# Attention weights, keys and queries turned by VectorE through DRAM, with all transfers of turned tiles issued by GpSimd

## The chip, the cores and the metric

The kernel runs on one core of one Trainium2 chip. The metric is the device time of one execution in microseconds (us). The engines of the core work beside each other, each in the order of its own instructions: TensorE (PE) multiplies matrices into PSUM banks, VectorE (DVE) and ScalarE (ACT) do the elementwise work, GpSimd (POOL) does small things, and SyncE (SP) issues loads. ACT, SP and now POOL also issue transfers (DMAs), which run on 16 DMA engines.

## What is computed

A backbone of two layers over 256 latent rows (4 grid rows of 64) and 256 context rows, with 2048 channels, in float32. The first layer has 16 attention heads beside 32 heads of a state-space scan (SSD), the second a short gated convolution. What the change touches is the attention of the first layer:

```python
def rms_norm(x, g):
    xf = x.astype(jnp.float32)
    y = xf * lax.rsqrt(jnp.mean(xf * xf, axis=-1, keepdims=True) + EPS)
    return (y * g.astype(jnp.float32)).astype(x.dtype)
...
    q = rms_norm(heads(cols(p, COL_Q, NA_WIDTH, 0), NA_HEADS, NA_HEAD_DIM), q_norm_g)
    k = rms_norm(heads(cols(p, COL_K, NA_WIDTH, 0), NA_HEADS, NA_HEAD_DIM), k_norm_g)
...
        s_lat = jnp.einsum('bqhd,bkhd->bhqk', qr, kb).astype(jnp.float32) * scale + bias.astype(jnp.float32)
        s_lat = jnp.where(mask, s_lat, -jnp.inf)
        s_ctx = jnp.einsum('bqhd,bkhd->bhqk', qr, k_ctx).astype(jnp.float32) * scale
        pr = jax.nn.softmax(jnp.concatenate([s_lat, s_ctx], axis=-1), axis=-1).astype(v.dtype)
...
    ya = neighbourhood_attention(q, k, v, k_ctx, v_ctx, rpb).reshape(b, seq, NA_WIDTH)
    ya = ya * jax.nn.silu(cols(p, COL_GATE_A, NA_WIDTH, 0))
```

Each head has 256 queries, 512 keys and a width of 128. Its 256 x 512 weights are taken times the values, the result times a SiLU gate.

## The kernel before

Every weight of the model is read once, in tiles of 128x1024 floats that SP loads into one of the `raw` buffers. ACT rounds a tile to `wH` (L423), DVE takes the rest as `wL` (L430), and PE multiplies three times, high by high, high by low and low by high (L198, the helper `mm`). Three pairs of `wH` and `wL` exist, so a pair can only be made over when PE is done with an older one. The input projection of the first layer runs through its columns in four stretches, each with four heads and two groups of the scan, then come the output projection, the second layer's input projection and its output projection.

Beside this stream stand generators: one for the keys or queries of four heads (`kq_gen`), one per head (`head_gen`), some per SSD group (`make_x`, `group_gen`), and one for the modulation's matrix-vector product (`gemv_gen`, on DVE, L820, from loads named `in_ada_w`). A planner, the class `Plan`, keeps a clock for each engine from a table of costs. While the stream of matmuls is written out, `pump` lets a generator go on as soon as its next instruction's inputs are ready by these clocks; so the table sets the order in which the work of the generators stands between that of the stream. What is written is a fixed order for each engine; nothing is reordered on the chip, and an engine whose next instruction waits does nothing behind it.

PE needs operands with the summed index on the 128 partitions. So K, Q and the attention weights have to be turned. Before, PE does it in steps of 128x128 (`turn`, L202, a multiplication with the identity that lands in a PSUM bank):

- `kq_gen` norms four tiles of 128x512 of K (two of Q) with DVE (L962), has each turned by four of PE's instructions, and copies the bank to `KT` with ACT (L979) or times the norms' gains to `QT` with DVE (L981).
- `head_gen` splits K and Q of the head in high and low parts, has the scores of 128 queries at a time multiplied (`kH,qH` and so on), adds the bias and takes the maximum on DVE (L1036), the exponential on ACT (L1041), divides on DVE (L1046), has 4 turns on PE, then splits the turned bank into `PH` (ACT, L1082) and `PL` (DVE, L1084). With `PH`, `PL` and the values PE makes the weighted sum.
- At the end of `group_gen` two 128x128 matmuls of a matrix of ones and a diagonal spread 256 norm factors `r` over the partitions; the factors come from a power on POOL (L1437).

The second layer already turns in another way: a row tile is written to DRAM (`trd`) by ACT's queue, fetched back in four transfers that place blocks of 32 on their partitions (`fetch`, L212), and DVE turns inside each 32x32 block (L217, STREAM_TRANSPOSE).

The results of heads and groups go to DRAM (`mixd`), and `mix_gen` reads them back for the output projection.

## Time and profile before

| | us |
|---|---|
| median of 3 runs | 1801.51 (1799.98 to 1804.06) |
| profiled execution | 1802.22 |
| its span, first to last instruction | 1800.3 |
| TensorE matmuls busy | 1760.2 |
| VectorE busy | 1283.5 |
| ScalarE busy | 785.7 |
| GpSimd busy | 31.1 |
| mean granted TensorE clock | 0.998 of full |

The span is shown in 40 slices of 45 us, each digit the busy share in tenths:

```profile
PE   6999999999999999999999999999999999999998
DVE  5566777878686867685875787787657777767555
DMA  9987654576656556655574566768757888878774
```

PE is busy in nearly every slice. The first two slices wait for the first loads, the last one holds the end of the output. DMA is the share in which the 16 DMA engines were busy: it is full at the start and between 0.5 and 0.7 during the attention (about 200 to 1150 us), and near 0.8 in the second layer (about 1370 us on).

### The profile page before, as it was taken

The page shows a single profiled execution, that of the slowest core. Times are in us where ns is not written, and L with a number is a line of the kernel's source. Part 1 is how long each engine was busy: PE and PEld are TensorE (multiplying, and loading weights), DVE is VectorE, ACT ScalarE, POOL GpSimd, SP SyncE. Part 2 cuts the span into 40 slices and gives each one's busy share as a digit, 9 for nine tenths or more (in the row PEclk, how much of TensorE's full clock was granted, in tenths as well). Part 3 has the DMA queues.
Part 4 walks back from the last instruction along what each step waited for, and adds up shares of the span by engine and source line. Part 5 has one row for each costly group of instructions (what it writes and reads, how often), then busy time and mean ns, then how long its engine had stood idle before and what let it go on. Part 6 is the DMA issues. An engine that isn't in the chain of part 4 may idle for free.

```text
span 1800.3 us, 25545 instructions
## 1 busy us (share of the span) xinstructions
PE 1760.2 (98%) x9545; PEld 1469.2 (82%) x9545; DVE 1283.5 (71%) x2049; ACT 785.7 (44%) x1354; POOL 31.1 (2%) x28
## 2 busy tenths in 40 slices
PE   6999999999999999999999999999999999999998
PEld 4677888889888879888878898788877888878887
DVE  5566777878686867685875787787657777767555
ACT  5323544436252455242454343554445444434442
POOL 0000100001000000000001000000000000000000
PEclk9999999999999999999999999999999999999999
DMA  9987654576656556655574566768757888878774
GB/s 347 340 291 254 194 168 126 156 206 194 211 161 190 162 174 204 191 158 167 172 219 120 163 188 194 232 209 295 273 184 232 260 278 268 270 237 265 220 220 167
DMA packets 260220, 385.23 MB, mean 214 GB/s; under 512 B 33424, under 2 KB 113008, under 8 KB 260096
## 3 DMA queue, kind: packets, MB, share of 16 engines
q1 hardware_dynamic: 239792, 366.64, 64.8%
q10 hardware_dynamic: 20304, 16.96, 3.1%
q8 instruction: 75, 1.23, 0.3%
q14 instruction: 49, 0.40, 0.1%
HBM read 372.89 MB, written 11.96 MB: 214 GB/s over the span
## 4 chain that ended last, share of the span: by engine, by line
PE 89%; DMA 4%; DVE 4%; issue 1%; ACT 1%; SPq 0%; POOL 0%; ACTq 0%; POOLq 0%; DVEq 0%
PE bank L198 86%; PE bank L202 3%; DMA raw<-in_ada_w 2%; DVE wL L430 2%; DMA tmp<-dram_csr 1%; DVE acc L820 0%; DMA raw<-in_w_in 0%; DMA Dg<-dram_trd 0%; ACT wH L423 0%; DMA tmp<-in_x 0%; DMA xs<-in_x 0%; DVE hL L769 0%; DVE tmp L1398 0%; DVE tmp L1217 0%; DMA Du<-dram_trd 0%
## 5 line engine op out<-in xcount | busy, mean ns | idle before, releaser
L423 ACT CAST wH<-raw 128x1024 fp32r<-128x1024 f32 (+1 forms) x440 | 459.5, 1045 | 707.4 <-PE bank L198 606.5
L430 DVE TENSOR_TENSOR wL<-raw,wH 128x1024 fp32r<-128x1024 f32 (+1 forms) x440 | 530.5, 1212 | 225.9 <-ACT wH L423 224.1
L198 PE MATMUL bank<-hH,wH 128*128 128x256 f32 (+1 forms) x1040 | 342.7, 330 | 0.9 <-ACT wH L423 0.9
L198 PE MATMUL bank<-hL,wH 128*128 128x256 f32 (+1 forms) x1040 | 336.8, 324 | 0.0
L198 PE MATMUL bank<-hH,wL 128*128 128x256 f32 (+1 forms) x1024 | 331.3, 324 | 1.5 <-DVE wL L430 1.5
L198 PE MATMUL bank<-wH,h 128*128 128x512 f32 x1024 | 318.7, 392 | 2.1 <-DVE h L1662 1.7
L198 PE MATMUL bank<-wH,hH 128*128 128x512 f32 x640 | 257.2, 402 | 4.8 <-ACT hH L763 2.6
L820 DVE SCALAR_TENSOR_TENSOR acc<-raw,csil,acc 128x512 f32<-128x512 f32 x256 | 191.7, 749 | 91.0 <-DMA raw<-in_ada_w 74.0
L198 PE MATMUL bank<-wL,hH 128*128 128x512 f32 x640 | 249.8, 391 | 0.3 <-DVE wL L430 0.3
L198 PE MATMUL bank<-wH,hL 128*128 128x512 f32 x640 | 249.5, 390 | 0.1
L198 PEld LDWEIGHTS bank<-wH,h 128*128 128x128 f32 x1024 | 193.0, 189 | 44.3 <-DVE h L1662 3.0
L198 PEld LDWEIGHTS bank<-hH,wH 128*128 128x128 f32 x1040 | 197.6, 190 | 18.7 <-issue 2.0
L198 PEld LDWEIGHTS bank<-hL,wH 128*128 128x128 f32 x1040 | 197.7, 190 | 15.6
L198 PEld LDWEIGHTS bank<-hH,wL 128*128 128x128 f32 x1024 | 194.5, 190 | 17.8 <-DVE wL L430 2.5
L198 PE MATMUL bank<-wL,h 128*128 128x512 f32 x512 | 200.7, 392 | 5.4 <-DVE wL L430 5.4
L198 PE MATMUL bank<-wH,mix 128*128 128x512 f32 x512 | 162.7, 393 | 0.0
L198 PEld LDWEIGHTS bank<-wH,hH 128*128 128x128 f32 x640 | 120.2, 188 | 35.3 <-issue 6.5
L198 PEld LDWEIGHTS bank<-wH,hL 128*128 128x128 f32 x640 | 120.1, 188 | 25.6 <-DVE hL L769 0.6
L198 PEld LDWEIGHTS bank<-wL,hH 128*128 128x128 f32 x640 | 120.2, 188 | 24.8 <-DVE wL L430 1.1
L198 PEld LDWEIGHTS bank<-wL,h 128*128 128x128 f32 x512 | 96.6, 189 | 27.1 <-DVE wL L430 6.9
L198 PEld LDWEIGHTS bank<-wH,mix 128*128 128x128 f32 x512 | 96.1, 188 | 20.8 <-issue 0.9
L198 PE MATMUL bank<-wL,mix 128*128 128x512 f32 x256 | 99.8, 390 | 0.0
(257 smaller groups left out, 1754.4 us busy)
## 6 DMA issues: line engine op xcount, KB each, us to landing
raw<-in_w_in SPq DMA_DIRECT2D x209, 512.0 KB, 3.8
raw<-in_ada_w SPq DMA_DIRECT2D x163, 512.0 KB, 4.7
raw<-in_sc_in SPq DMA_DIRECT2D x128, 512.0 KB, 4.4
raw<-in_w_out SPq DMA_DIRECT2D x64, 512.0 KB, 4.8
raw<-in_sc_out SPq DMA_DIRECT2D x32, 512.0 KB, 4.6
tmp<-dram_csr SPq DMA_DIRECT2D x32, 256.0 KB, 6.2
PT<-in_ada_w SPq DMA_DIRECT2D x14, 512.0 KB, 8.0
yi<-in_ada_w SPq DMA_DIRECT2D x8, 512.0 KB, 7.4
```

The source lines that it names most:

```text
L198: E(T.matmul(o, l, r, start=start, stop=stop, skip_group_check=True))
L202: E(T.transpose(o, i, ident if k == 128 else ident[:k, :k]))
L423: E(S.copy(H, v))
L430: E(V.tensor_tensor(out=Lo, in0=v, in1=H.bitcast(F32), op=ALU.subtract))
L820: E(V.scalar_tensor_tensor(out=acc, in0=v[:, j], scalar=csil[:, 2 * k + j:2 * k + j + 1], in1=acc, op0=ALU.mult, op1=ALU.add))
```

## The change

1. K and Q (`kq_gen`): the normed tile is written in blocks of 32 (`mixed`), sent to DRAM (`kqd`) by POOL, fetched back two tiles at a time into one buffer (`d_take`, in the place of `PT0`), and DVE turns it straight into `KT` or `QT`. The gains of the norms go into the split of Q.
2. Attention weights (`head_gen`): the exponential writes a new tile in blocks of 32, ACT divides, POOL writes to DRAM (`ptd`) and fetches, DVE turns in place, and `PH` and `PL` are each made by one instruction of 128x1024. The buffer is the same as that of K and Q, one user at a time (`dfree`). The factor 0.5 goes into the multiplication with the gate.
3. All writes and fetches of turned tiles, those of the second layer (`trd`) too, are issued by POOL in place of ACT.
4. The planner counts 1200 ns per transfer issued by POOL and 3000 ns more for a transfer to or from DRAM tiles, and a generator can ask for 1000 ns more of readiness ("DVE+", "ACT+"); the gemv's multiply and the turns do.
5. The SSD norm's factors are spread by a turn of the factor itself in place of a matmul with a diagonal.
6. Smaller: the gemv starts with a multiply and adds its bias at the end, with no memset; a mix whose place is free already is split straight into it (`place`); the residual's generators start when heads and groups are done.

```diff
         for k in ko:
-            s = max(s, 0.0 if e == "PE" else self.w[k] + 60, self.r[k] + 60)
+            s = max(s, 0.0 if e == "PE" or op == "DMACopy" else self.w[k] + 60, self.r[k] + 60)
...
-            self.t[e] = s + 450
+            self.t[e] = s + (1200 if e == "POOL" else 450)
...
+            if any(a.tensor.name.startswith("dram") for a in ins + outs):
+                done = free = done + 3000
...
         for b in range(4):
-            E(DMA2.dma_start(dst[32 * b:32 * b + 32].rearrange("p t (a x) -> p (t a) x", a=4),
+            E(G.dma_start(dst[32 * b:32 * b + 32].rearrange("p t (a x) -> p (t a) x", a=4),
                              bass.AP(tensor=src.tensor, offset=src.offset + 128 * b, ap=[[512, 32], [32 * 512, n], [1, 128]])))
...
-        rdy = plan.ready(aps)
+        rdy = plan.ready(aps) + (1000 if late else 0)
...
-                yield W_("DVE", RAW["gem", n, k][1], acc)
+                yield W_("DVE+", RAW["gem", n, k][1])
...
     def put_mix(i, o):
+        if free_rows[0] > i % 16:
+            yield W_("ACT", o)
+            place(i, o)
+            give(free_h, o)
+            return
...
+        for t in range(nt):
+            yield W_("DVE", stat)
+            kn = tmp()
+            E(V.tensor_tensor(out=mixed(kn), in0=plain(ps[t]),
+                              in1=stat[:, 4 * t:4 * t + 4].unsqueeze(2).unsqueeze(3).to_broadcast([128, 4, 4, 32]), op=ALU.mult))
             if banked:
                 give(free_b, ps[t])
...
+            yield W_("POOL", kn)
+            E(G.dma_start(src[t * 128:(t + 1) * 128], kn))
+            give(free_t, kn)
...
-            for h in range(4):
-                turn(pt[:, h * 128:(h + 1) * 128], kns[t][:, h * 128:(h + 1) * 128])
...
+        for t in range(0, nt, 2):
+            yield when(lambda: dfree[0])
+            Dk = d_take(f"kqD_{key}{a}{t}")
+            yield W_("POOL", src[t * 128:(t + 2) * 128])
+            fetch(Dk, src[t * 128:(t + 2) * 128])
+            for k in range(2):
+                yield W_("DVE+", Dk)
+                blocks(dst[:, :, (t + k) * 128:(t + k + 1) * 128], Dk[:, k])
+            dfree[0] = True
...
+            ex = sps[qt] = tmp()
+            E(S.activation(mixed(ex), plain(sp), AF.Exp, bias=s4[:, 2 + qt:3 + qt], scale=1.0, accum_out=s4[:, 4 + qt:5 + qt]))
...
+            E(S.mul(sps[qt], sps[qt], s4[:, 6 + qt:7 + qt]))
+            yield W_("POOL", sps[qt])
+            E(G.dma_start(ptd[hd, qt * 128:(qt + 1) * 128], sps[qt]))
...
+        Dt = d_take(f"D{hd}")
+        got.add(("d", hd))
+        yield W_("POOL", ptd[hd])
+        fetch(Dt, ptd[hd])
+        for qt in range(2):
+            yield W_("DVE+", Dt)
+            turned = Dt[:, qt].rearrange("p (a k j) -> p a k j", a=4, k=4)
+            E(V.transpose(turned, turned))
...
+        E(S.copy(flat(PH), Dt.rearrange("p t x -> p (t x)")))
+        yield W_("DVE", PH)
+        E(V.tensor_tensor(out=flat(PL), in0=Dt.rearrange("p t x -> p (t x)"), in1=flat(PH).bitcast(F32), op=ALU.subtract))
+        dfree[0] = True
...
-            mm(Rb[:, t * 128:(t + 1) * 128], ONES, dg[:, t * 128:(t + 1) * 128], t == 0, True)
...
+            turn(Rb[:, t * 128:(t + 1) * 128], r2[:, t:t + 1].to_broadcast([128, 128]))
...
-            yield W_("AQ", ut)
-            E(DMA2.dma_start(trd[2 * i, t * 128:(t + 1) * 128], ut))
+            yield W_("POOL", ut)
+            E(G.dma_start(trd[2 * i, t * 128:(t + 1) * 128], ut))
```

How the order of the instructions moves is seen best at three places. The first is PE in the first stretch of the stream, where the SSD group's inputs are turned (`make_x`, 4 turns of one tile at a time) while a head is under way. Before:

```order
L198 MATMUL bank_123<-wH_137,hL_1133 128x512
L202 MATMUL bank_129<-const,tmp_112 128x128 x4
L198 MATMUL bank_127<-wH_137,hH_1128 128x512
L198 MATMUL bank_127<-wL_140,hH_1128 128x512
L198 MATMUL bank_127<-wH_137,hL_1133 128x512
L202 MATMUL bank_130<-const,tmp_113 128x128 x4
L198 MATMUL bank_123<-wH_137,hH_1135 128x512
```

And in the changed kernel, at `make_x` of the same stretch:

```order
L200 MATMUL bank_129<-wH_138,hL_373 128x512
L204 MATMUL bank_130<-const,tmp_104 128x128 x4
L200 MATMUL bank_125<-wH_136,hH_559 128x512
L200 MATMUL bank_125<-wL_139,hH_559 128x512
L200 MATMUL bank_125<-wH_136,hL_564 128x512
L200 MATMUL bank_124<-tmp_107,Btmt 128x512
L200 MATMUL bank_124<-tmp_109,Btmt 128x512
L200 MATMUL bank_127<-tmp_113,Btmt 128x256 x2
L204 MATMUL bank_123<-const,tmp_112 128x128 x4
```

In the first piece `tmp_112` and `tmp_113` are a head's weights; such rows of 4 turns stand 56 times for K, Q and heads. In the second only `make_x`'s own turns are left, and no row for K, Q or weights stands anywhere on PE.

The second place is POOL in the same stretch. `statk` and `statq` are the norms of K and Q, `r_0` and `r_1` those of the SSD groups. Before, that is all POOL has to do:

```order
L572 TENSOR_TENSOR statk<-statk,const 128x16
L572 TENSOR_TENSOR statq<-statq,const 128x8 x2
L1437 TENSOR_TENSOR r_0_1705<-r_0_1705,const 128x2
L572 TENSOR_TENSOR statk<-statk,const 128x16
L1437 TENSOR_TENSOR r_1_1706<-r_1_1706,const 128x2
```

Now, from the weights of the third head on:

```order
L1078 DMA dram_ptd<-tmp_108 128x512
L1078 DMA dram_ptd<-tmp_113 128x512
L1078 DMA dram_ptd<-tmp_105 128x512
L1078 DMA dram_ptd<-tmp_110 128x512
L214 DMA D_3242<-dram_ptd 32x8x128 x4
L1467 TENSOR_TENSOR r_0_1705<-r_0_1705,const 128x2
L576 TENSOR_TENSOR statk<-statk,const 128x16
L214 DMA D_3567<-dram_ptd 32x8x128 x4
L996 DMA dram_kqd<-tmp_110 128x512
L996 DMA dram_kqd<-tmp_104 128x512
L996 DMA dram_kqd<-tmp_112 128x512
L996 DMA dram_kqd<-tmp_107 128x512
```

The powers of the norms now stand behind transfers, and a fetch of a head (`D`) waits for that head's writes to land before POOL goes on.

The third place is DVE in the same stretch, where a head's weights are split. Before, for the first head:

```order
L1045 RECIPROCAL s_0_1693<-s_0_1693 128x1
L1046 TENSOR_SCALAR tmp_112<-tmp_112,s_0_1693 128x512
L1045 RECIPROCAL s_0_1693<-s_0_1693 128x1
L1046 TENSOR_SCALAR tmp_104<-tmp_104,s_0_1693 128x512
L829 COPY rowb<-bank_125 128x128
L430 TENSOR_TENSOR wL_140<-raw_135,wH_137 128x1024
L1036 ISA tmp_105,s_1_1694<-bank_129,bias_214 128x512
L1036 ISA s_1_1694 128x1
L1039 TENSOR_SCALAR s_1_1694<-s_1_1694 128x1
L1084 TENSOR_TENSOR PL<-bank_130,PH 128x4x128
```

Now, for the third head (`D_3242` is its buffer):

```order
L1109 STREAM_TRANSPOSE D_3242<-D_3242 128x512
L434 TENSOR_TENSOR wL_141<-raw_133,wH_138 128x1024
L1109 STREAM_TRANSPOSE D_3242<-D_3242 128x512
L1465 TENSOR_SCALAR r_0_1705<-bank_126 128x2
L1443 TENSOR_TENSOR half_122<-bank_129,yi 128x256
L1445 TENSOR_TENSOR half_122<-half_122,sz 128x256
L826 SCALAR_TENSOR_TENSOR acc<-raw_134,csil,acc 128x512 x2
L1476 SCALAR_TENSOR_TENSOR half_115<-half_115,small,bank_126 128x256
L1476 SCALAR_TENSOR_TENSOR half_121<-half_121,small,bank_126 128x256
L434 TENSOR_TENSOR wL_139<-raw_135,wH_136 128x1024
```

The divisions (L1046) and the parts from the bank (L1084) have left DVE's order, and turns that wait for a transfer stand in it, with the `wL` of the stream behind them.

## The prediction

> **What bounds the kernel now.** I read the busy shares first, then the chain of waits, then the groups and the order of time of TensorE (PE) itself.

> ```profile
> PE 1760.2 (98%) x9545; PEld 1469.2 (82%) x9545; DVE 1283.5 (71%) x2049; ACT 785.7 (44%) x1354; POOL 31.1 (2%) x28
> PE 89%; DMA 4%; DVE 4%; issue 1%; ACT 1%; SPq 0%; POOL 0%; ACTq 0%; POOLq 0%; DVEq 0%
> ```

> PE is busy for 98% of the span, and 89% of the chain that ended last is PE's own work. So the time is PE's work plus the waits in which PE stands still. What leaves PE leaves the span, as long as no new wait of PE takes its place.

> The list of PE's waits from 130 us on, behind the start, is short:

> ```profile
> PE bank L198 <- DVE wL L430: 6.9, 6, 4.4
> PE bank L198 <- DVE tmp L1401: 2.5, 3, 1.3
> PE bank L198 <- DVE h L1662: 1.7, 2, 1.4
> PE bank L198 <- ACT Vt L989: 1.4, 1, 1.4
> ```

> The columns are us in total, times and longest us. The whole list sums to 14.3 us (four rows below 1 us are left out). One wait of 4.4 us is the largest, and the order of time of DVE, the windows and ACT's queue show where it comes from:

> ```profile
> 1581.53 2.53 ACTq L212 DMA_DIRECT2D Du<-dram_trd  x4
> 1552.74 1.54 DVE L820 SCALAR_TENSOR_TENSOR acc<-raw,csil,acc 128x512 f32<-128x512 f32 x2 [4.23 <-DMA raw<-in_ada_w]
> 1590.66 1.54 DVE L820 SCALAR_TENSOR_TENSOR acc<-raw,csil,acc 128x512 f32<-128x512 f32 x2 [5.00 <-DMA raw<-in_ada_w]
> 1584.00:1586.00 2.00, 2.00 (x11) 1.65 (x10) 1.65 (x2) 1.05 (x1) 0.00 (x0) 1.00 1.04 206
> 1589.00:1590.00 1.00, 0.00 (x1) 0.00 (x0) 0.00 (x0) 0.86 (x1) 0.00 (x0) 1.00 0.20 78
> 1591.00:1592.00 1.00, 0.00 (x0) 0.00 (x0) 0.96 (x2) 0.00 (x0) 0.00 (x0) 0.72 0.00 0
> 1593.00:1594.00 1.00, 0.61 (x2) 0.52 (x3) 1.00 (x2) 0.00 (x0) 0.00 (x0) 0.50 0.70 141
> 1597.00:1598.00 1.00, 1.00 (x4) 0.81 (x3) 0.00 (x0) 0.00 (x0) 0.00 (x0) 0.50 1.04 391
> 1598.00:1599.00 1.00, 1.00 (x6) 0.76 (x5) 0.00 (x0) 0.53 (x1) 0.00 (x0) 0.86 1.05 408
> ```

> DVE works in order. While it waits 5.0 us for a load, the weight parts wL (L430) queue behind it, and PE runs dry from 1589.0 to 1593.4. The third number from the end of a window's row is PE's granted clock: it falls to 0.50 in the gap and is back only at 1598.3. So PE then works 4.9 us at half rate and loses 2.4 us more. This stall costs 4.4 + 2.4 = 6.8 us. DVE's other wait, 4.2 us, costs PE only 0.8 us. **DVE's cover is about 4 us; beyond it a stall costs about 7.** [...]

> **What the change takes from PE.** It removes the turns of K, Q and of the attention weights: 16 x 4, 8 x 4 and 32 x 4, 224 in all. The group has all turns of tmp tiles, and the order of time shows four of them between weight matmuls:

> ```profile
> L202 PE MATMUL bank<-const,tmp 128*128 128x128 f32 x324 | 45.9, 273 | 0.2 <-ACT KT L979 0.2
> 349.73 0.39 PE L198 MATMUL bank<-wH,hL 128*128 128x512 f32 x1
> 349.96 0.60 PE L202 MATMUL bank<-const,tmp 128*128 128x128 f32 x4
> 350.32 0.48 PE L198 MATMUL bank<-wH,hH 128*128 128x512 f32 x1
> 350.63 0.39 PE L198 MATMUL bank<-wL,hH 128*128 128x512 f32 x1
> 350.86 0.39 PE L198 MATMUL bank<-wH,hL 128*128 128x512 f32 x1
> ```

> A 128x512 matmul starts every 0.23 us. After the turns at 349.96 the second next starts at 350.63, so the first counts from 350.40: four turns cost 0.44 us, 0.11 each (the mean of 273 ns overlaps with its neighbours). 224 x 0.11 = **24.6 us**. In the SSD norm 16 matmuls of 128x128 become 16 turns. PE runs such a matmul in two passes, each as long as a turn (277 against 273 ns), and the 44 passes of this row are the 22 matmuls of that name:

> ```profile
> L198 PE MATMUL bank<-half,const 128*128 128x128 f32 (+1 forms) x44 | 7.0, 277 | 0.1
> ```

> 32 passes go and 16 turns come: 16 x 0.11 = **1.8 us**. Together 26.4 us, with no work of PE added: the matmuls on PH and PL are as many as before.

> **What it gives to DVE and ACT.**

> ```profile
> L1084 DVE TENSOR_TENSOR PL<-bank,PH 128x512 fp32r<-128x512 f32 x32 | 21.9, 684 | 5.8 <-ACT PH L1082 5.4
> L1046 DVE TENSOR_SCALAR tmp<-tmp,s 128x512 f32<-128x512 f32 x32 | 15.6, 487 | 1.1
> L981 DVE TENSOR_SCALAR QT<-bank,gqk 128x512 f32<-128x512 f32 x8 | 5.8, 743 | 0.8 <-PE bank L202 0.8
> L810 DVE MEMSET acc<- 128x512 f32 x16 | 7.8, 485 | 0.9
> L217 DVE STREAM_TRANSPOSE cg<-Dg 128x512 f32<-128x512 f32 x8 | 5.2, 688 | 1.5 <-DMA Dg<-dram_trd 1.5
> L430 DVE TENSOR_TENSOR wL<-raw,wH 128x1024 fp32r<-128x1024 f32 (+1 forms) x440 | 530.5, 1212 | 225.9 <-ACT wH L423 224.1
> L423 ACT CAST wH<-raw 128x1024 fp32r<-128x1024 f32 (+1 forms) x440 | 459.5, 1045 | 707.4 <-PE bank L198 606.5
> L1082 ACT CAST PH<-bank 128x512 fp32r<-128x512 f32 x32 | 18.3, 588 | 29.0 <-PE bank L202 28.2 <-DVE half L1104 0.7
> L979 ACT COPY KT<-bank 128x512 f32<-128x512 f32 x16 | 8.9, 589 | 8.7 <-PE bank L202 8.7
> L613 ACT ACTIVATE xs<-xs,rx 128x512 f32<-128x512 f32 x8 | 5.5, 717 | 4.6 <-POOL rx L572 4.6
> ```

> DVE loses 21.9 + 15.6 + 5.8 + 7.8 = 51 us. It gets 56 turns of 0.69 us (row L217) and 16 PL of 128x1024 at 1.21 us (row L430): 58 us. ACT loses 27 us, and gets 16 PH at 1.05 (row L423) and 32 products at 0.72 (row L613): 40 us. Both also wait most of the time. I cost this at nothing, because PE's work hides it. Where that cover is thin, in the window from 855 to 900 us where DVE is busy for 40.1 of 45 us, it is rival B:

> ```profile
> 855.00:900.00 45.00, 44.48 (x288) 39.45 (x287) 40.14 (x61) 19.31 (x26) 0.00 (x0) 1.00 0.58 171
> ```

> **What waits for the new transfers.** 28 tile groups (12 of K and Q, 16 heads) now make the way that only the 8 groups of dram_trd made, and all 36 go by GpSimd (POOL): 72 writes and 144 fetches, where POOL issued none. POOL's own price per transfer is in no row. The nearest are ACT's:

> ```profile
> dram_trd<-tmp ACTq DMA_DIRECT2D x16, 256.0 KB, 4.7
> Du<-dram_trd ACTq DMA_DIRECT2D x16, 128.0 KB, 8.1
> L212 ACTq DMA_DIRECT2D Du<-dram_trd x16: 310/463/721, 1404.0 to 1674.0; - x16
> L1041 ACT ACTIVATE tmp<-tmp,s 128x512 f32<-128x512 f32 x32 | 23.2, 726 | 11.9 <-DVE s L1039 11.8
> L1036 DVE CUSTOM_DVE_ANT_1 tmp<-bank,bias 128x512 f32<-128x512 f32 x16 | 11.0, 685 | 3.5 <-PE bank L198 3.5
> ```

> From a head's second score to its weighted sum: maximum 0.7, Exp 0.7, product 0.7, write 4.7, four issues 1.9, landing 8.1, two turns 1.4, PH 1.0, PL 1.2, together 20.4 us. As the changed order stands, the shortest such stretch on PE, head 4, holds 117 matmuls of 128x512: 117 x 0.23 = 26.9 us. Heads 6 and 8 have 123, 28.3 us; the rest have more. So even the tightest head has 6.5 us for queues and for a slower POOL, and PE doesn't wait there. PE's own wait for POOL is the SSD norm's power, once for each of 8 groups. It now stands behind transfers in POOL's order, and a turn of PE waits for it:

> ```profile
> L1437 POOL TENSOR_TENSOR r<-r,const 128x2 f32<-128x2 f32 x8 | 7.1, 887 | 388.2 <-DVE r L1435 388.2
> ```

> At its tightest place nine matmuls of 128x512 lie between the norm's sum and that turn, 2.1 us, and the power needs 0.9. Four issues of 0.46 ahead of it, 1.9 us, would cost PE 0.7 us, and 5 us in all eight; they lie so close in few of them, and I count this among the new waits.

> The 8 old groups cost PE 6.8 + 0.8 = 7.6 us in the two places above, 0.95 each. At that price the 28 new ones would cost 26.6 us, which is the upper bound; the lower is nothing. I take 4 us: the stall at 1589 came out of a window whose DMA share (second number from the end) was 1.04, and the attention's stretch has 0.58 in the window from 855 us, nearer to the free end. Of the old 7.6 us I take back 5: the change lets gemv's multiply wait for its load a further 1 us in the plan, which brings a wait of 5.0 near that of 4.2, and takes the fetches from ACT. The bounds are 0 and 7.6.

> **Sum.** The profiled execution took 1802.2 us (its span of 1800.3 and 1.9 around it), 0.7 above the median of 1801.5. 1802.2 - 24.6 - 1.8 - 5 + 4 = 1774.8, and against the median **1774 us**.

> **Rivals.**

> *B, given back in part.* DVE's order takes in the turns and its waits grow in the stretches where it is nearly full; a few stalls of PE come back. Two stalls of 6.8 us give 1774 + 14 = 1788; with the upper bound of the new waits, 26.6 in place of 4, it is 1797. For it: the 40.1 of 45 us. Against: PE waits 14.3 us in all today.

> *C, slower: POOL's transfers land too late.* Place: the turn on DVE, in order ahead of wL, and the power behind the transfers on POOL. [...] For it: POOL has not been tried in this trace. Against: the cover of 6.5 us and more on PE. [...]

> *D, faster still.* All of PE's 14.3 us of waits and the 2.4 us of half clock go: 1801.5 - 26.4 - 16.7 = 1758.

> *E, no change.* The turns are gone from PE's order, so this needs the new waits to eat just the gain: 1798 to 1805.

> **How the numbers follow.** Forecast (1764 to 1783) 0.55, B (1783 to 1798) 0.20, D 0.07, E 0.05, C 0.13. 0.2% is 3.6 us, about what a measurement can tell from no change. Faster 0.55 + 0.20 + 0.07 = 0.82, same 0.05, slower 0.13. The range 1758 to 1798 takes in the forecast, B and the price of D.

> **What would show it.** Right: the row of turns of tmp at x100, PE's instructions at 9305 (9545 - 224 - 32 + 16), PE's list of waits near 14 us, no window with a clock below 1. DVE's turns of D waiting over 4 us for their transfers, with clocks of 0.50 behind, would show C; a DVE at 90% in the windows between 225 and 1150 us and short waits of PE for wL would show B. It is wrong above all if POOL's transfers take much longer than ACT's, or if POOL's power keeps PE waiting in the eight norms.

## The result and the profile after

| | before | after |
|---|---|---|
| median, us | 1802.78 (4 runs, 1799.98 to 1809.95) | 1781.62 (4 runs, 1778.70 to 1786.17) |
| ratio | | 0.9874 [0.9855, 0.9894] |
| profiled execution, us | 1802.22 | 1781.03 |

The change takes 21.2 us, where 27 to 28 were forecast; 1781.62 lies in the forecast's own range of 1764 to 1783, at its upper end. The busy times and the chain that ended last, from the changed kernel's page:

```profile
PE 1736.7 (98%) x9305; PEld 1445.1 (81%) x9305; DVE 1278.5 (72%) x2017; ACT 799.0 (45%) x1354; POOL 160.3 (9%) x245
PE 71%; issue 10%; DMA 8%; DVE 7%; POOL 2%; ACT 1%; SPq 1%; DVEq 0%; ACTq 0%; POOLq 0%
```

its groups of instructions (busy time, mean ns, then idle time ahead and what ended it):

```profile
L204 PE MATMUL bank<-const,tmp 128*128 128x128 f32 x100 | 15.0, 273 | 0.7 <-ACT tmp L1150 0.7
L204 PE MATMUL bank<-const,r 128*128 128x128 f32 x16 | 3.0, 272 | 0.0
L1467 POOL TENSOR_TENSOR r<-r,const 128x2 f32<-128x2 f32 x8 | 7.9, 990 | 150.7 <-DVE r L1465 150.7
```

and its span with the mean granted clock:

```profile
core 0: 1779.2 us, clock 0.997
```

PE's share of the chain went from 89% to 71%, and DMA, DVE and "issue" stand there for it: four rows of 1% each are transfers of turned tiles, and the largest DMA row, 3%, is the loads of the matrix-vector product (2% before). That alone says nothing of the time, as PE is still busy for 98%. PE has 9305 instructions, as counted ahead, and its group of turns of tmp tiles has x100 for x324. PE's busy time fell by 23.5 us and the span by 21.1.

A span can be split in three. Idle time is the span less PE's busy time. Busy time at clock c is counted as a loss of (1 - c) of its length, an estimate: in the changed kernel three 128x512 matmuls take 1.28 us at a clock of 0.50 (1495.41 to 1496.69) and 0.68 us at 1.00 (1491.14 to 1491.82). Summed over windows of 0.2 us that is what the half clock cost. (It is counted where PE is busy alone: the mean clock of the whole span also holds half clock over idle time, which would then count twice.) The rest is PE's work at the full clock.

| profiled execution, us | span | PE busy | half clock | PE's work | idle + half clock |
|---|---|---|---|---|---|
| before | 1800.3 | 1760.2 | 2.4 | 1757.8 | 42.5 |
| after | 1779.2 | 1736.7 | 5.1 | 1731.6 | 47.6 |

So PE's work fell by 26.2 us, and 5.1 came back as idle time and half clock. Of these 42.5 and 47.6 us some 26 are idle time of the start and the last slice in both. The waits of PE from 130 us on, in the changed kernel (us in total, times, longest):

```profile
PE bank L200 <- DVE wL L434: 4.4, 6, 1.8
PE bank L200 <- ACT qH L1085: 2.7, 2, 1.6
PE bank L200 <- DVE tmp L1431: 2.3, 1, 2.3
PE bank L200 <- DVE qL L1088: 0.8, 2, 0.6
PE bank L200 <- DVE PL L1115: 0.7, 2, 0.4
```

The one wait of 4.4 us is gone. In its place are short ones, and some come from turned tiles: qH and qL are the split of the first turned queries of a batch, PL that of the weights. Here is one of them, in the order of time of POOL, DVE, ACT and PE:

```profile
716.38 1.74 POOL L214 DMA_DIRECT2D kqD_K<-dram_kqd  x3 [10.83 <-DVE rowb L835]
721.55 0.58 POOL L214 DMA_DIRECT2D kqD_K<-dram_kqd  x1 [3.43 <-issue]
...
724.25 1.30 DVE L219 STREAM_TRANSPOSE KT<-kqD_K 128x512 f32<-128x512 f32 x2 [6.50 <-DMA kqD_K<-dram_kqd]
...
725.58 0.62 ACT L1084 CAST kH<-KT 128x512 fp32r<-128x512 f32 x1 [3.06 <-DVE KT L219]
...
726.67 0.50 PE L200 MATMUL bank<-kH,qH 128*128 128x512 f32 x1 [1.15 <-ACT qH L1085]
```

POOL issues three fetches, and the fourth only after 3.43 us of idle time. DVE's turn needs all four and waits 6.50 us for them. ACT makes kH from the turned keys and qH behind it, and PE's first score waits 1.15 us for qH. The fetches start right behind DVE's turns of the pair of tiles before (714.68 to 715.98), which use the same buffer; a second buffer wasn't tried. "issue" says that POOL waited for nothing that the profile can name; the run ring2048 below shows what it is.

### The profile page after: what moved, and what is told of

It reads as the page before. It is cut to its first block, busy times and chain, and to the rows that moved or that the text cites. A ratio compares the mean times of both kernels' runs of the same rounds, so it can differ in the third digit from the quotient of the medians.

```text
span 1779.2 us, 25400 instructions
## 1 busy us (share of the span) xinstructions
PE 1736.7 (98%) x9305; PEld 1445.1 (81%) x9305; DVE 1278.5 (72%) x2017; ACT 799.0 (45%) x1354; POOL 160.3 (9%) x245
## 4 chain that ended last, share of the span: by engine, by line
PE 71%; issue 10%; DMA 8%; DVE 7%; POOL 2%; ACT 1%; SPq 1%; DVEq 0%; ACTq 0%; POOLq 0%
PE bank L200 70%; DMA raw<-in_ada_w 3%; DVE wL L434 2%; PE bank L204 1%; DMA raw<-in_w_in 1%; DMA dram_trd<-tmp 1%; DVE acc L826 1%; DMA bias<-dram_rpbs 1%; DMA kqD_K<-dram_kqd 1%; DMA D<-dram_ptd 1%; ACT wH L427 1%; DMA Du<-dram_trd 1%; POOL statk L576 0%; POOL kqD_K L214 0%; POOL Dg L214 0%
## 5 line engine op out<-in xcount | busy, mean ns | idle before, releaser
L427 ACT CAST wH<-raw 128x1024 fp32r<-128x1024 f32 (+1 forms) x440 | 459.4, 1045 | 650.9 <-PE bank L200 553.2
L826 DVE SCALAR_TENSOR_TENSOR acc<-raw,csil,acc 128x512 f32<-128x512 f32 x240 | 179.3, 747 | 41.1 <-DMA raw<-in_ada_w 37.3
## 6 DMA issues: line engine op xcount, KB each, us to landing
dram_ptd<-tmp POOLq DMA_DIRECT2D x32, 256.0 KB, 4.1
D<-dram_ptd POOLq DMA_DIRECT2D x64, 128.0 KB, 4.9
tmp<-dram_csr SPq DMA_DIRECT2D x32, 256.0 KB
```

Of the source, the lines that this page charges most:

```text
L427: E(S.copy(H, v))
L826: E(V.scalar_tensor_tensor(out=acc, in0=v[:, j], scalar=csil[:, 2 * k + j:2 * k + j + 1], in1=acc, op0=ALU.mult, op1=ALU.add))
```

## The experiments

All ratios are to the kernel before, taken beside it on the same chip; its medians lay between 1802.8 and 1806.7 us. A difference of two ratios is turned into us with 1804.

### TensorE's work put back without use

```diff
         po = bank()
+        for _ in range(14):
+            turn(po[:, :128], ident)
         for kt in range(4):
```

> The changed kernel, with 14 turns of the identity by TensorE ahead of each head's weighted sum, 224 in all, written to the bank that the sum then overwrites: TensorE's removed work is put back as work whose result nothing uses, and every transfer, VectorE turn and plan number stays. If the gain is TensorE's work (224 x 0.11 = 24.6 us on a TensorE that is 98% busy), the time goes from 1781.6 to 1803-1808 and TensorE's busy time from 1736.7 to about 1761. If the turns of before were covered by waits that TensorE had anyway and the gain comes from the other edits, it stays at 1780-1787.

1804.41 us, ratio 1.0000 [0.9982, 1.0019]. The 224 turns cost 22.7 +- 4.9 us over the changed kernel, 0.10 each, and the busy time went to 1761.2, PE's work to 1755.1. The order of all engines was planned anew around them. So PE had no room for them: the turns of before weren't covered by anything.

### The turns given back, the rest kept

```diff
-            yield W_("POOL", sps[qt])
-            E(G.dma_start(ptd[hd, qt * 128:(qt + 1) * 128], sps[qt]))
...
-        fetch(Dt, ptd[hd])
...
+            pt = bank()
+            for kt in range(4):
+                turn(pt[:, kt * 128:(kt + 1) * 128], sps[qt][:, kt * 128:(kt + 1) * 128])
```

and the same for keys and queries.

> The changed kernel with the turns of keys, queries and attention weights given back to TensorE (and their copies out of the banks as before), while the transfers of the gated MLP stay on GpSimd, the plan keeps its higher prices and margins, and the norm, the mixed rows and the matrix-vector product stay changed. If the gain is TensorE's turns, it loses 24.6 us and gets back the waits that the 28 new groups caused (of the 16.2 us of TensorE's waits those on turned keys, queries and weights, at most 8): 1797-1806. If the gain comes from the other edits: 1780-1787.

1796.65 us, ratio 0.9953 [0.9938, 0.9969], just below the lower end of what the first theory expected. The turns' part is 0.0079 of the ratio, 14.3 +- 4.5 us; the other edits bring 8.5 +- 2.8, and which of them how much wasn't tried, but for the margins below. In the profiled execution (span 1795.6, PE busy 1758.3, half clock 3.6) PE's work is 1754.7 and idle + half clock 40.9. Against the changed kernel the turns are 23.1 us of PE's work, and 6.7 us come back with the new transfers.

### The plan's prices

Both prices as before:

```diff
-            self.t[e] = s + (1200 if e == "POOL" else 450)
+            self.t[e] = s + 450
...
-                done = free = done + 3000
+                pass
```

> The changed kernel with the plan's prices of transfers as before: 450 ns for an issue on GpSimd where the change has 1200, and no 3000 ns on what goes through DRAM. The margin of 1000 ns on turns stays. If the order matters (VectorE's turns then stand some 3 us earlier in its row than their data land, 36 groups, and what stands behind the turn waits too), VectorE's waits on turned tiles rise from 23 us to over 80, TensorE meets more of them, windows with a clock of 0.5 come up, and the time is 1795-1850. If VectorE's slack covers this anyway: 1779-1786.

1903.38 us, ratio 1.0536 [1.0510, 1.0562]: slower than before the change, and beyond the expected range. Then each price alone. Without the landing's 3000 ns:

> The changed kernel without the 3000 ns that the plan puts on transfers through DRAM; GpSimd's issues keep their 1200 ns. With both prices as before the time was 1903.4 us, 121.8 above the changed kernel, and VectorE waited 141.0 us for turned tiles (74.3 + 25.2 + 20.9 + 20.6) for about 23. Fetches land 4.9 us after issue in the middle and the plan without the 3000 ns counts about 2.5, so if it is the landing that the order must know, this run has most of the loss: 1860-1900, with waits of VectorE on turned tiles above 90 us. If the time of the issue on GpSimd (four fetches of 0.59 us and up to 5.7 us ahead of the fourth) is what it must know, the loss is small here: 1782-1805.

1911.59 us, ratio 1.0588 [1.0557, 1.0619]. Without the issue's 1200 ns:

> The changed kernel with 450 ns for GpSimd's issues as before; the 3000 ns on transfers through DRAM stay. Four fetches are then planned 3 us too early. If the landing is what the order must know: 1781-1795, waits of VectorE on turned tiles 25-50 us. If the issue is: 1840-1900, waits above 90 us. If both loss parts add up, this run and the one without landing price lie about half way each, near 1840.

1792.97 us, ratio 0.9928 [0.9908, 0.9949]. So it is the landing: without it all of the loss is there, and without the issue's price only 9.7 us. The two don't add up half and half. In the run without the landing's price, DVE's waits for turned tiles, the order of time of POOL, DVE and PE at one place, and the windows behind it (PE's busy time first, its clock the third number from the end):

```profile
DVE D L1109 <- DMA D<-dram_ptd: 65.7, 11, 7.8
DVE KT L219 <- DMA kqD_K<-dram_kqd: 21.6, 6, 6.0
DVE u L219 <- DMA Du<-dram_trd: 21.0, 4, 6.0
DVE QT L219 <- DMA kqD_Q<-dram_kqd: 14.5, 4, 7.5
```

```profile
526.37 1.76 POOL L214 DMA_DIRECT2D D<-dram_ptd  x3 [8.05 <-DVE PL L1115]
527.02 0.28 DVE L835 TENSOR_TENSOR rowb<-bank,adab 128x128 f32<-128x128 f32 x1
...
532.36 0.59 POOL L214 DMA_DIRECT2D D<-dram_ptd  x1 [4.22 <-DMA dram_mrow<-rowb]
...
533.68 0.29 PE L200 MATMUL bank<-PL,vH 128*128 128x256 f32 x1
535.12 0.71 DVE L1109 STREAM_TRANSPOSE D<-D 128x512 f32<-128x512 f32 x1 [7.82 <-DMA D<-dram_ptd]
535.75 1.18 DVE L434 TENSOR_TENSOR wL<-raw,wH 128x1024 fp32r<-128x1024 f32 x1
...
538.63 0.68 DVE L1123 TENSOR_TENSOR vL<-Vt,vH 128x512 fp32r<-128x512 f32 x1
...
539.37 0.58 PE L200 MATMUL bank<-PH,vL 128*128 128x256 f32 x1 [5.40 <-DVE vL L1123]
```

```profile
537.00:538.00 1.00, 0.00 (x0) 0.00 (x0) 0.96 (x3) 0.00 (x0) 0.00 (x0) 0.92 0.01 2
538.00:539.00 1.00, 0.00 (x0) 0.00 (x0) 1.00 (x2) 0.00 (x0) 0.00 (x0) 0.50 0.56 80
...
543.00:544.00 1.00, 1.00 (x4) 0.81 (x3) 1.00 (x1) 1.00 (x3) 0.00 (x0) 0.50 0.51 131
544.00:545.00 1.00, 1.00 (x5) 0.76 (x4) 1.00 (x3) 0.41 (x1) 0.00 (x0) 0.67 0.92 313
```

The turn of the next head's D stands in DVE's row ahead of vL of the head that PE is at. DVE waits 7.82 us, PE has no vL and stands for 5.40, and the clock is at 0.50 until some 544.7.

Over the whole run (span 1911.5, PE busy 1781.0, half clock 41.5) idle + half clock is 172.0 for 47.6: 124 of the 132 us are stalls. The other 8 stand as PE's work, 1739.5 for 1731.6, and why isn't known. The 3000 ns stand on the other transfers through DRAM too (mixed rows, for one); but DVE's waits on turned tiles alone rose by about 106 us (the four rows and 5.8 for cg, 128.6, against 23.1).

POOL's fourth fetch waits 4.22 us behind the third here, as it waits 3.43 us in the changed kernel above, so the wait of 7.82 us also holds what `ring2048` below takes away; the two edits weren't run together. Two of PE's waits in this run, 11.0 us in all, are for POOL's power in the norm, which the prediction named as a way to be wrong.

### GpSimd or ScalarE as the place of issue

```diff
-            E(G.dma_start(dst[32 * b:32 * b + 32]...
+            E(DMA2.dma_start(dst[32 * b:32 * b + 32]...
...
-            yield W_("POOL", sps[qt])
-            E(G.dma_start(ptd[hd, qt * 128:(qt + 1) * 128], sps[qt]))
+            yield W_("AQ", sps[qt])
+            E(DMA2.dma_start(ptd[hd, qt * 128:(qt + 1) * 128], sps[qt]))
```

> The changed kernel with every write and fetch of turned tiles issued by ScalarE's queue instead of GpSimd's (the plan then counts 450 ns for an issue; landing price and margins stay). In the trace of before, ScalarE's issue took 0.46 us and its fetches landed 8.1 us after it in the middle; GpSimd's in the changed kernel take 0.59 us and land after 4.9 to 6.2. If the later landing counts, VectorE's waits on turned tiles rise above 60 us and the time is 1795-1840; if ScalarE's row, which also makes each wH, is held up by 144 issues, PE's waits for wH rise as well. If GpSimd is no better a place: 1779-1786.

1794.38 us, ratio 0.9938 [0.9918, 0.9959], 11.5 +- 5.1 us slower than with POOL, and not because of later landings: DVE's waits for turned tiles fell, to 14.0 us from 24.9 (its rows for KT, D, u and cg). What shows is ACT's row held up, though PE then waits for wL and tmp, not for wH. ACT's queue, ACT, DVE and PE at the place of the longest stall:

```profile
304.44 3.67 ACTq L214 DMA_DIRECT2D D<-dram_ptd  x4
308.15 1.05 ACT L427 CAST wH<-raw 128x1024 fp32r<-128x1024 f32 x1 [4.36 <-DMA raw<-in_ada_w]
309.11 1.44 ACT L1241 ACTIVATE tmp<-bank,cbh,cwh 128x512 f32<-128x512 f32 x2
309.91 5.32 DVE L1247 SCALAR_TENSOR_TENSOR tmp<-bank,cwh,tmp 128x508 f32<-128x508 f32 x7 [4.90 <-ACT tmp L1241]
316.42 0.58 PE L200 MATMUL bank<-hH,wL 128*128 128x256 f32 x1 [5.17 <-DVE wL L434]
```

Four fetches hold ACT's row for 3.67 us. ACT's next cast starts 0.04 us behind the last of them, so it was the issues that ACT was at in its 4.36 us, though the row names the load that came last. DVE waits 4.90 us for the tmp behind that cast, and PE waits 5.17 us for the wL behind DVE's work on that tmp; with half clock behind it that is some 6.9 of the 11.5 us. POOL has little else in its row, so such a hold stops few others there. PE's waits for wL rose to 10.1 us from 4.4.

But the edit also took the plan's price of an issue from 1200 to 450 ns, and on POOL alone that cost 9.7 +- 5.1 us. With 450 ns on both, ACT is 1.8 us slower by the ratios, which is within the noise. ACT with 1200 ns wasn't run, so it isn't shown that ACT is the worse place.

### Room for GpSimd's descriptors

```diff
-    sb.tile([128, 224], F32, tag="pad", name="pad", bufs=1)
+    sb.tile([128, 8], F32, tag="pad", name="pad", bufs=1)
...
-    nc = bacc.Bacc("TRN2", target_bir_lowering=False, num_devices=1, dynamic_dma_scratch_size=1024)
+    nc = bacc.Bacc("TRN2", target_bir_lowering=False, num_devices=1, dynamic_dma_scratch_size=2048)
```

> The changed kernel with twice the scratch for the descriptors of GpSimd's transfers (2048 bytes for 1024; 864 bytes of an unused pad tile are given up for the room). In the changed kernel's trace GpSimd's fetches show 102.4 us of waits named issue, nearly all ahead of the fourth fetch of a group. If these are waits for room among the descriptors, they fall below 25 us, VectorE's waits on turned tiles (10.5 + 7.4 + 5.2 us) fall below 10, and where they carried TensorE's short stalls, the time falls to 1773-1779. If the fetches are late for another reason (landing, the writes ahead of them), the waits stay above 80 us and the time is 1780-1783. If the waits go but hid beside other work, the waits fall and the time stays at 1780-1783.

1783.50 us, ratio 0.9888 [0.9865, 0.9910]: no gain, the third case. What POOL's fetches wait for, in the source view of their line, first after, then with 2048 bytes:

```profile
  issue: 102.4, 46
```

```profile
  issue: 1.8, 6
```

Of the 102.4 us, 93.8 stood ahead of the fourth fetch, in 34 of 36 groups; two more groups have such a wait under another name. They are gone, so they were for room. DVE's waits on turned tiles fell to 9.7 us from 24.9, but those for the matrix-vector product's loads rose to 48.6 from 37.3, in the same order of instructions on every engine. PE's short stalls stand elsewhere (gaps of 2.3 us near 238 us, 2.1 near 410 and 1.5 near 765, in place of 1.6 near 471, 2.3 near 1115 and 1.8 near 1493), and idle + half clock is 46.8 us. The late fourth fetch starts single stalls, as at 724 us, but it isn't what the kernel's time hangs on.

### The margins

`"DVE+"` and `"ACT+"` ask for some time over what the plan says; the edit is the number, `(1000 if late else 0)`. One run takes the `+` from the matrix-vector product's step alone, and one raises the landing's 3000 ns to 4500 instead.

> The changed kernel without the margin of 1000 ns that turns on VectorE, steps of the matrix-vector product and copies of mixed rows get over what the plan says; prices stay as changed. VectorE's turns then stand up to 1 us earlier. If time given to transfers has to be enough and what is short goes to TensorE (price as in the plan of before: 122 us for about 4 us on each of 36 groups, some 30 us for 1 us if that were even), it is 1785-1812. If 3000 ns and 1200 ns already cover the landings, as medians of 4.9 and 5.5 us say for half the fetches, 1778-1784.

> The changed kernel with the margin of 1000 ns taken from the steps of the matrix-vector product alone; VectorE's turns and the copies of mixed rows keep theirs. Without all margins it was 22.2 us slower (1803.8 against 1781.6), VectorE's waits for the product's loads were 91.3 us for 37.3, and those on turned tiles 34 us for 25. If the product's loads are what the margin is for, as in the stall of before at 1589, nearly all of that comes here: 1795-1804, with those waits above 70 us. If the turned tiles are: 1780-1788.

> The changed kernel with a margin of 2500 ns in place of 1000 for turns, steps of the matrix-vector product and copies of mixed rows. Given back TensorE's turns the kernel took 1796.7, so the turns bring 15.0 of the 20.6-24.6 us that TensorE is freed from, and 6-10 us go to new waits. If those are transfers that land within 2.5 us behind their planned time, most of them go: 1772-1778, VectorE's waits on turned tiles below 12 us, those for the product's loads below 15. If what is left of the stalls comes from the places where they fall and moves about with every new order, 1779-1786, and the waits fall without the time.

> The changed kernel with 4500 ns in place of 3000 for transfers through DRAM; margins of 1000 ns stay. If fetches that land later than planned cause the stalls left over: 1773-1779, VectorE's waits on turned tiles (25 us) below 8. If the longer planned way (a write and a fetch, 3 us more for each group) only moves the stalls to what waits for the turned tiles on TensorE: 1780-1790, with those waits gone all the same.

| | median, us | ratio | idle + half clock, us |
|---|---|---|---|
| no margin | 1803.84 | 0.9990 [0.9972, 1.0008] | 63.9 |
| none for the matrix-vector product | 1794.06 | 0.9954 [0.9936, 0.9972] | 54.3 |
| 1000 ns (the changed kernel) | 1781.62 | 0.9874 [0.9855, 0.9894] | 47.6 |
| 2500 ns | **1770.88** | 0.9815 [0.9803, 0.9828] | 38.9 |
| 1000 ns, landing 4500 for 3000 | 1774.17 | 0.9834 [0.9821, 0.9847] | 40.0 |

Without the margins the change is worth nothing. Of their 20.9 +- 4.8 us, 14.4 +- 4.8 belong to the matrix-vector product's steps, which load straight from HBM and have nothing to do with turns. DVE's waits for these loads, without their margin, after, and with 2500 ns:

```profile
DVE acc L826 <- DMA raw<-in_ada_w: 80.1, 50, 5.5
```

```profile
DVE acc L826 <- DMA raw<-in_ada_w: 37.3, 22, 4.5
```

```profile
DVE acc L826 <- DMA raw<-in_ada_w: 21.2, 11, 3.7
```

In the kernel before, which has no margin, these waits sum to 74.0 us, and one of them made the stall at 1589; in the run without any margin they sum to 91.3 us. The margin of 2500 ns is faster than both kernels, by 10.6 +- 4.2 us against the changed one, a little more than expected, though the waits fell less than expected: those on turned tiles to 13.5 us from 24.9, where below 12 was expected, and those above to 21.2, where it was below 15. The landing at 4500 ns brings 7.2 +- 4.2 us, within its range, with waits on turned tiles of 8.5 us where below 8 was expected. Whether it is the turned tiles or the product's loads that matter, the last run tells:

> The kernel with TensorE's turns given back (1796.7 with a margin of 1000 ns, 15.0 above the changed kernel) and the margin of 2500 ns, with which the changed kernel took 1770.9. Here the margin can act on the product's loads, the mixed rows and the gated MLP's turns, but on no turned keys, queries and weights. If what the margin took away in the changed kernel were waits on those turns, it does little here: 1792-1798, and the turns of TensorE are worth 21-27 us at this margin, close to the 20.6-24.6 of the sum. If it took away waits of the product's loads and the like, it does the same here: 1784-1789, and the turns are worth 13-18 us at any margin.

1787.21 us, ratio 0.9889 [0.9870, 0.9909]: the second case. The margin of 2500 ns brings 11.5 +- 4.5 us here too, without one turned key, query or weight. The turns are worth 13.3 +- 4.2 us at this margin and 14.3 +- 4.5 at 1000. The profiled execution (span 1785.1, PE busy 1753.9) has 31.2 us of idle time and no half clock while PE is busy; against the 38.9 above, 7.7 us come back with the new transfers, no less than the 6.7 at 1000 ns. I had expected the margin to work on the turned tiles, and that has fallen. Each number gives a new order on all engines, so some of every difference here is where the stalls happen to fall.

## Why the prediction came out as it did

**PE bounds: right.** In eight of the ten kernels with these turns off PE its work at the full clock is 1730.5 to 1735.7 us, at spans from 1769 to 1798; in the two without the landing's price it is 1739.5. In the three where PE has the turns, or dummies in their place, it is 1753.9 to 1755.1. The rest of each span is idle time and half clock.

**The 24.6 us of turns: right, a little high.** The two pairs of kernels with and without them give 23.1 and 23.4 us of PE's work, the dummies 22.7 by the times: 0.10 a turn for 0.11. All of the change took 26.2 us of work from PE, for 26.4 in the sum. That this is so near is partly luck: the turns are 1.5 us below the sum's 24.6, and the other edits, 3.1 us, are above the 1.8 that the sum gave to the norm. Which of them brought the rest wasn't tried.

**Nothing for DVE and ACT: right.** ACT's busy time rose by 13.3 us, forecast 13. DVE's fell by 5.0 where the sum had 7 more; among what it had left out are the norm's 16 products with the diagonal. PE's waits for wL are 4.4 us in six pieces, where they were 6.9 before, so rival B's sign didn't come.

**POOL's transfers: the sum right, its two terms not.**

The first row is the source view of POOL's fetches (ns, smallest, median and largest), the second the list of transfers with the median time from issue to landing.

```profile
L214 POOL DMA_DIRECT2D D<-dram_ptd x64: 582/588/627, 284.5 to 1200.6; - x64
```

```profile
D<-dram_ptd POOLq DMA_DIRECT2D x64, 128.0 KB, 4.9
```

An issue takes 0.59 us for the 0.46 taken from ACT, and the fetch lands after 4.9 us for 8.1. But with the wait for room ahead of the fourth fetch, four issues take 5.0 us for a head in the middle, where the sum had 1.9. From the first issue to the last landing it is 9.5 us (7.7 to 11.7 over the 16 heads) for the sum's 10.0, because the two errors cancel. No issue was slow: the smallest and the largest of 64, 582 and 627 ns, lie 8% apart, while DVE is busy for 72% of the span. The power on POOL took 990 ns for 887, and PE's turns of it (const,r) waited 0.0 us, where 5 us were held possible.

**The heads: right, the keys: left out.** PE waited 0.7 us for PL. The way of turned keys and queries to the first score of a batch wasn't worked out, and PE's waits for qH and qL, 3.5 us, are there.

**The balance of stalls: wrong by 6 us.** The forecast took 5 us back from the old stalls and put 4 to the new ones, -1 in sum. The profiled executions show +5.1, and that is nearly all of the 6.2 us by which 1781.03 is above the sum of 1774.8. The new stalls were put too low: they cost 6.7 us by the profiles and 23.1 - 14.3 = 9 +- 4.5 by the medians. For the old ones it isn't settled: by the profiles they gave back 1.6 (42.5 to 40.9), by the medians some 5 of the 8.5 +- 2.8 us that the edits other than the turns brought. Both lie within the bounds given, 0 to 7.6 and 0 to 26.6.

The price behind the upper bound, 0.95 us for each old group, was also read from the wrong waits. Both old stalls came from DVE's waits for the loads of the matrix-vector product; for turned tiles DVE waited only 2.1 us before:

```profile
DVE acc L820 <- DMA raw<-in_ada_w: 74.0, 50, 5.0
DVE cg L217 <- DMA Dg<-dram_trd: 1.5, 1, 1.5
DVE u L217 <- DMA Du<-dram_trd: 0.6, 1, 0.6
```

So neither the 4 us nor its bound was worked out from waits like the new ones, and that the result still fell into the range owes something to luck.

**What the forecast didn't see is what its 4 us rested on.** It took the new order as given and never priced the plan's 3000 ns. Rival C had the right place, but the transfers needn't be slow: a turn that stands in DVE's row before its data lands is enough. The 124 us of stalls without the landing's price are 18 of the forecast's stalls of 6.8 us, and C's sign, turns of D that wait over 4 us with clocks of 0.50 behind, is what that run shows. And of the sign "no window with a clock below 1" nothing is left: the changed kernel has clocks of 0.50 near 28, 762 and 1496 us, and PE's waits sum to 16.2 us for "near 14".

## What to carry to other kernels

Where an order is fixed ahead, a transfer's time in the plan is a term of the kernel's time: leaving 3 us of landing out turned a gain of 21 us into a loss of 106 here. So for a change that adds waits on transfers, find the engine whose row they stand in, read the landing time from the trace, and give the plan more than the median; then try a wider margin, here worth another 10.6 us, and try it apart from the change, since most of it may belong to something else. Look also at who else stands in the row of the engine that issues: four fetches held ScalarE's row for 3.67 us, though by the times it wasn't shown to be the worse place.

## What the runs showed of the hardware that was not expected

GpSimd's fourth fetch of a group stood. With 1024 bytes of scratch three of these fetches of 128 KB went out in a row in 30 of 36 groups, in six the third waited too, and the waits named issue sum to 102.4 us. With 2048 they sum to 1.8 us, and the four fetches of the keys at 722.02 go out in a row, in 2.32 us. An issue itself took 0.58 to 0.64 us in both.

In the changed kernel's trace the length of a gap doesn't decide whether the clock drops. Two places of the changed kernel, each window 1 us, PE's busy time first and its clock third from the end:

```profile
1493.00:1494.00 1.00, 0.00 (x0) 0.00 (x0) 1.00 (x2) 0.52 (x1) 0.00 (x0) 1.00 0.00 0
1494.00:1495.00 1.00, 0.55 (x2) 0.49 (x3) 1.00 (x2) 0.00 (x0) 0.00 (x0) 1.00 0.00 0
1495.00:1496.00 1.00, 1.00 (x4) 0.78 (x3) 1.00 (x2) 0.00 (x0) 0.00 (x0) 0.53 0.67 117
...
1498.00:1499.00 1.00, 1.00 (x5) 0.82 (x4) 0.00 (x0) 0.14 (x1) 0.00 (x0) 0.77 0.97 350
...
1115.00:1116.00 1.00, 0.00 (x0) 0.00 (x0) 0.67 (x3) 0.12 (x1) 0.00 (x0) 1.00 0.89 310
1116.00:1117.00 1.00, 0.15 (x2) 0.15 (x4) 0.97 (x4) 0.58 (x2) 0.00 (x0) 1.00 0.41 152
1117.00:1118.00 1.00, 1.00 (x8) 0.75 (x7) 1.00 (x2) 0.00 (x0) 0.00 (x0) 1.00 0.27 98
```

Behind a gap of 1.79 us before 1494.45 the half clock came, when PE was already at work again, for 3.4 us (from 1495.05 to 1498.46); behind one of 2.34 us before 1116.85 it didn't.

Where the line lies isn't shown. The gap of 2.34 us falls on two steps of the grid, with 1.66 us in the first. But a gap of 1.74 us from 1583.99, which lies whole in one step, brought no drop either, and three gaps of 0.92 us in all, in the step before 761.18, did.
